# A hand-written VectorE and ScalarE order in the memory block's output projection, and another order of the FFN's PSUM banks

## The chip, the cores and the metric

The kernel runs on one core of one Trainium2 chip. The metric is the device time of one execution in microseconds (us). Before the change it was measured in three runs: 1961.02, 1964.95 and 1965.83 us, median 1964.95 us. Inside a core TensorE (PE) multiplies matrices into PSUM, VectorE (DVE), ScalarE (ACT) and GpSimd (POOL) work element by element, and SyncE (SP) issues the DMAs. Each engine executes its own instructions in a fixed order and waits on semaphores for the others.

## The reference

The reference is one decoder layer over 1024 prompt tokens and 32 sample tokens (1056 columns): a mixer, a cross-attention into 256 memory tokens, and a gated FFN with a short convolution, each added to the residual. What matters here is the end of the second and the start of the third:

```python
def mem_attend(h, mk, mv, w_mq, g_mq, w_mo):
    ...
    o = jnp.einsum('nhtm,nmhd->nthd', p, mv.astype(q.dtype)).reshape(n, t, MEM_WIDTH)
    return o @ w_mo                                   # 512 -> 1024

xp = xp + mem_attend(rms_norm(xp, g_mem_x[l]), mk, mv, w_mq[l], g_mq[l], w_mo[l])
y, buf = conv_ffn(rms_norm(xp, g_ffn[l]), ..., w_up[l], w_conv[l], b_conv[l], w_down[l])

def conv_ffn(h, buf, w_up, w_conv, b_conv, w_down):
    gate, val = jnp.split(h @ w_up, 2, axis=-1)       # 1024 -> 2 x 2816
    ...
```

All of it is float32. A float32 product is made of three products of rounded operands: each operand is split into a high part (a rounding cast) and a low part (what the cast dropped).

## The kernel before, in words

**The output projection (`out`, L1709 to L1725).** The 1056 columns are taken in two halves of 528 (`h` = 0, 1), the 1024 output rows in eight blocks of 128, `m = 4 * e + j`. One call `out(h, j, w, y)` makes two blocks (`e` = 0, 1), so the stage has 16 products; this text numbers them 0 to 15 in the order of the program: half 0 with j = 0, 1, 2, 3 (products 0 to 7), half 1 with j = 1, 2, 3, 0 (products 8 to 15). Product k is 24 matmuls of 264 columns into one of three PSUM buffers `y` of two banks each, so product k + 3 needs the buffer of product k. Then follow, on other engines:

- sum k: VectorE adds the PSUM result to the old residual, `res`, L1721 (three buffers, loaded by SP at L1715);
- SP stores the new residual to DRAM, `yd`, L1722;
- ScalarE scales it by the FFN's norm gain into `y` (L1723), and squares it (L1517 or L1520, in `square`); GpSimd adds the square to the sum of squares `ya` (L1521). The sum of squares starts anew at products 0 and 8.

The weights of one `j` (`weight(j)`, L1598) are loaded and split by `stream`: one cast on ScalarE (L190), one subtraction on VectorE (L191), 128x1024 each. Three pairs of buffers hold them, so j = 3 comes after product 1 is done, and j = 0 of the second half after product 9.

**The operand steps (`operands`, L1789).** The FFN multiplies with a Strassen-Winograd scheme: seven products of quarter blocks in the place of eight. For each half and each pair of j (d = 0: j = 0, 1; d = 1: j = 2, 3) seven operands (`FORMS`) are made from the scaled residual, four of them differences. One operand is: a difference for t1, t3, t2, t4 (VectorE, L1797, in place in `y`), the cast to the high part (ScalarE, L190) and the subtraction that gives the low part (VectorE, L191), all 128x528. That makes four blocks of seven operands, 11 VectorE instructions and 7 casts each. In this text block a is half 0, d = 0; b is half 0, d = 1; c is half 1, d = 1; d is half 1, d = 0. Blocks b and c share the buffer `y1[1]`.

**The first FFN weights (`weights`, L1816).** From two loads of `w_up` GpSimd makes four sums `s12`, `s34` (L1836 to L1840); casts and subtractions give the high and low parts of `raw[0]`, `s12`, `s34` (the last subtraction on GpSimd, L1825) and of `a22` (L1843, L1844).

**The first FFN block (`block`, L1865).** Per half seven products of 12 matmuls: A, X (t2), X (b21), F (t1, t3), E (b22, t4). Before the second X buffer can be used again, VectorE must have made `z` from the first (L1874). The second half's first product in the program as it runs is X of `t21`, which needs the operand t2 of blocks c and d.

**What sets the order.** A planner orders the instructions when the program is built: an instruction goes to its engine when its inputs are ready in the planner's own timing, the earlier one in the program first. Inside `manual_schedule(engines=...)` the named engines keep the order of the program; instructions from behind such a block may be placed into its gaps. Before the change the whole stage was left to the planner. PSUM has eight banks; a pool gives them out by the order in which its tags are first asked for. The projection's pool has `y` in banks 0 to 5 and `st` in bank 6; product 15 lies in banks 0 and 1. The FFN's pool had A in banks 0 and 1, X in 2 and 3, F in 4 and 5, E in 6 and 7.

Of the kernel before, what the change touches and what calls it, by code (L numbers as in the profile page):

```python
# [5 lines left out]
F32 = mybir.dt.float32  # L6
# [3 lines left out]
ALU = mybir.AluOpType  # L10
# [3 lines left out]
P = 128  # L14
# [10 lines left out]
HT, QT = 528, 264  # L25
# [128 lines left out]
class Net:  # L154
# [1358 lines left out]
    def square(self, p, acc, x, m):  # L1513
        nc = self.nc
        n = x.shape[1]
        if m == 0:
            nc.scalar.activation(acc, x, AF.Square)  # L1517
        else:
            sq = self.t(p, [P, max(n, 384)], F32, "sqx", 3 if n <= 384 else 2)[:, :n]
            nc.scalar.activation(sq, x, AF.Square)  # L1520
            nc.gpsimd.tensor_tensor(acc, acc, sq, ALU.add)  # L1521


    def mem_attention(self, xh, xl, r3):
        nc, tc, I, O = self.nc, self.tc, self.I, self.O
        pq = self.open("pq")
        pp = self.open("psa", space=PSUM)
# [20 lines left out]
        w, st = {}, {}  # L1548
# [149 lines left out]
        px = self.open("xo0", side="right")  # L1698
# [3 lines left out]
        y1 = [self.t(pc, [P, 2, 2, HT], F32, f"y{d}") for d in range(2)]  # L1702
        acc = self.t(self.pw, [P, 640], F32, "ya")
        pc0 = self.open("pc0", side="right")
        nc.gpsimd.memset(acc[:, HT:], 0.0)
        self.close("psa")
        pp = self.open("psm", space=PSUM)

        def out(h, j, w, y):  # L1709

            o = h * HT
            for e in range(2):
                m = 4 * e + j
# [7 lines left out]
                nc.vector.tensor_tensor(r, ps, r, ALU.add)  # L1721
                nc.sync.dma_start(self.y_dram[:, m, o : o + HT], res)  # L1722
                nc.scalar.activation(y[:, e, j % 2], res, AF.Copy, scale=self.col("g_ffn", m))  # L1723
                self.square(pc0, acc[:, :HT], res, count[0] % 8)
                count[0] += 1  # L1725

        count = [0]
        ys = self.t(pc0, [P, 2, 2, HT], F32, "y"), y1[1]
        for j in range(4):
            if j == 3:  # L1730
                w[j] = weight(j)
            out(0, j, w[j], ys[j // 2])
            if j % 2:
                self.operands(ys[j // 2], j // 2, ops[0], self.FORMS)
        r = self.t(self.pw, [P, 10], F32, "hr")

        def sums(h, st):
            for i in range(5):
                nc.tensor.matmul(st[:, i : i + 1], acc[:, i * P : i * P + P], self.ones[:, :1], start=True, stop=True)
            nc.scalar.copy(r[:, 5 * h : 5 * h + 5], st[:, :5])  # L1740

        sums(0, self.t(pp, [P, 512], F32, "st", 1))
        w[0] = weight(0)
        for j in (1, 2, 3, 0):
            out(1, j, w[j], y1[j // 2])
            if j in (3, 0):
                self.operands(y1[j // 2], j // 2, ops[1], self.FORMS[:3])
            if j == 2:
                first = self.weights(0, 1)
        self.close("pq")  # L1750
        self.close("pc0")
        px = self.open("xo2")
        rows = [self.t(px, [P, HT], F32, f"row{h}") for h in range(2)]
        for n in self.FORMS[3:]:
            form(px, 1, n)
        for d in (1, 0):
            self.operands(y1[d], d, ops[1], self.FORMS[3:])
        self.close("psm")
        self.close("pc")

        def norm(h, new):

            if h == 0:
                sums(1, new())
# [24 lines left out]
    def operands(self, y, d, ops, forms):  # L1789

        nc = self.nc
        b11, b12, b21, b22 = self.quarters(y)
        src = {"b11": b11, "b21": b21, "b22": b22, "t1": b11, "t3": b12, "t2": b22, "t4": b21}
        sums = {"t1": (b12, b11), "t3": (b22, b12), "t2": (b22, b11), "t4": (b21, b22)}
        for n in forms:
            if n in sums:
                nc.vector.tensor_tensor(src[n], *sums[n], ALU.subtract)  # L1797
# [16 lines left out]


    def weights(self, fa, fb, more=None):  # L1816

        nc, I, p = self.nc, self.I, self.pw

        def halves(src, eng=nc.vector):  # L1820
            self.nw += 1
            q = None if self.nw % 4 else more
            hi, lo = (self.t(q or self.wp, [P, 8, P], FR, x, 1 if q else None) for x in ("hi", "lo"))
            nc.scalar.copy(hi, src)  # L1824
            eng.tensor_tensor(lo, src, hi, ALU.subtract)  # L1825
# [10 lines left out]
        add(s12[:, :4], a21, a22, ALU.add)  # L1836
        add(s12[:, 4:], s12[:, :4], a11, ALU.subtract)
        w.update(zip(("s1", "s2"), halves(s12)))
        add(s34[:, :4], a11, a21, ALU.subtract)
        add(s34[:, 4:], a12, s12[:, 4:], ALU.subtract)  # L1840
        w.update(zip(("s3", "s4"), halves(s34, nc.gpsimd)))
# [4 lines left out]
        return w  # L1846

    def ffn(self, *a):
        self.ffn_up(*a)
# [2 lines left out]
    def ffn_up(self, ops, rows, norm, first):  # L1852

        nc, I, O = self.nc, self.I, self.O
        p = self.open("pf")
        pp = self.open("psf", space=PSUM)
        state = self.t(p, [P, NF, 16], F32, "state")
        nc.sync.dma_start(state, I["state"])
        conv = self.t(p, [P, NF, 18], F32, "conv")
        ocol, wcol = COL["b_conv"][0], COL["w_conv"][0]  # L1860
        def product(ps, a, b):
            pairs = lambda x: [(x[0][:, k], x[1][:, k]) for k in range(4)]
            self.mm3(ps, pairs(a), pairs(b))
# [87 lines left out]
        for q in range(NF // 2):  # L1951
            fs = 2 * q, 2 * q + 1
            w = self.weights(*fs, p) if q else first
# [4 lines left out]
            w = self.weights(NF + fs[0], NF + fs[1], p)  # L1958
# [128 lines left out]
```

## Time and profile before

| | |
|---|---|
| median of 3 runs | 1964.95 us |
| the profiled execution | 1963.94 us, span 1961.9 us from its first to its last instruction |
| TensorE busy | 1882.0 us, 96% of the span |
| VectorE busy | 1372.2 us, 70% |
| ScalarE, GpSimd busy | 902.1 us, 705.0 us |
| the output projection's first matmul | at 1167.87 us |
| the FFN's first matmul, `A` | at 1225.26 us |
| the first matmul of the FFN's second half, `X<-t21h` | at 1242.67 us |

A row of the timeline gives the start in us, the duration in us, the engine, the line, the operation, output and inputs, and in brackets how long the engine sat idle before it and which instruction released it. SPq is SyncE's queue of DMA issues. Each matmul row counts from its own start to the modelled end, so rows overlap; the distance of two starts is what one matmul takes of the engine. A row of windows gives the busy time of each engine in a stretch, and PEclk, the granted TensorE clock as a share of full speed.

### The profile page before, as it was taken

How to read it: one execution, taken by the hardware profiler on the slowest of the kernel's cores; microseconds unless marked ns; L12 is line 12 of the kernel's file. 1: busy time of each engine (PE TensorE's matmuls, PEld its weight loads, DVE VectorE, ACT ScalarE, POOL GpSimd, SP SyncE). 2: the span in 40 equal slices, each digit the busy share in tenths (PEclk: the TensorE clock that was granted, in tenths of full speed). 3: DMA queues.
4: the chain of work that ended last, by engine and by line, in shares of the span. 5: the costliest groups of instructions: out<-in, count | busy, mean ns of one | idle time of the engine just before them, and what ended most of it. 6: DMA issues, size and time to landing. Idle time of an engine off the chain costs nothing.

```text
span 1961.9 us, 40154 instructions
## 1 busy us (share of the span) xinstructions
PE 1882.0 (96%) x14556; PEld 1770.0 (90%) x14556; DVE 1372.2 (70%) x2949; ACT 902.1 (46%) x1880; POOL 705.0 (36%) x811
## 2 busy tenths in 40 slices
PE   5999899999999999999999998899999999999999
PEld 5999778768888989888899978899999999899999
DVE  8774867766777767777655668888888988832521
ACT  6334667666555555555533556433333333521311
POOL 5230401003544444444133015467677676100000
PEclk9999899999999999999999999899999999999999
DMA  5101100106865665654565145122222222754642
GB/s 202 50 5 49 57 1 2 61 14 184 223 181 162 176 176 170 173 166 136 172 186 180 37 152 184 40 78 79 86 66 77 88 75 90 213 171 128 200 124 66
DMA packets 130312, 229.42 MB, mean 117 GB/s; under 512 B 20449, under 2 KB 86850, under 8 KB 130114
## 3 DMA queue, kind: packets, MB, share of 16 engines
q1 hardware_dynamic: 129250, 225.81, 37.9%
q8 instruction: 115, 1.88, 0.4%
q10 hardware_dynamic: 864, 1.05, 0.2%
q14 instruction: 83, 0.68, 0.1%
HBM read 195.13 MB, written 31.66 MB: 116 GB/s over the span
## 4 chain that ended last, share of the span: by engine, by line
PE 67%; DVE 8%; issue 5%; DMA 4%; POOL 2%; ACT 1%; SPq 1%; POOLq 0%; DVEq 0%; ACTq 0%
PE s L184 14%; PE d L184 13%; PE b L184 7%; PE X L184 6%; PE F L184 6%; PE E L184 6%; PE A L184 3%; PE o L847 2%; PE tp L834 2%; PE tp L184 1%; DMA araw<-actd 1%; PE o L1277 1%; DMA cT<-cT 1%; DVE mx L1228 1%; PE tp L789 1%
## 5 line engine op out<-in xcount | busy, mean ns | idle before, releaser
L184 PE MATMUL s<-w2h,ch 128*128 128x288 f32 (+1 forms) x1024 | 305.9, 299 | 0.0
L184 PE MATMUL s<-w2h,cl 128*128 128x288 f32 (+1 forms) x1024 | 295.0, 288 | 2.8 <-POOL cl L1164 2.0
L184 PE MATMUL s<-w2l,ch 128*128 128x288 f32 (+1 forms) x1024 | 294.7, 288 | 0.0
L184 PE MATMUL d<-a,hi 128*128 128x264 f32 x1408 | 260.5, 286 | 3.4 <-DVE a L191 1.7
L184 PEld LDWEIGHTS d<-a,hi 128*128 128x128 f32 x1408 | 219.6, 189 | 5.2 <-DVE a L191 3.2
L184 PEld LDWEIGHTS s<-w2h,ch 128*128 128x128 f32 x1024 | 192.6, 188 | 19.1 <-issue 13.6
L184 PE MATMUL d<-a,lo 128*128 128x264 f32 x704 | 200.3, 285 | 0.0
L184 PEld LDWEIGHTS s<-w2h,cl 128*128 128x128 f32 x1024 | 192.4, 188 | 3.5 <-POOL cl L1164 2.3
L184 PEld LDWEIGHTS s<-w2l,ch 128*128 128x128 f32 x1024 | 192.8, 188 | 0.0
L1207 DVE TENSOR_REDUCE ss<-sq 128x16 f32<-128x1024 f32 x128 | 155.4, 1214 | 48.4 <-ACT sq L1204 48.2
L191 DVE TENSOR_TENSOR lo<-raw,hi 128x1024 fp32r<-128x1024 f32 (+1 forms) x71 | 83.3, 1174 | 131.3 <-ACT hi L190 131.2
L190 ACT CAST hi<-raw 128x1024 fp32r<-128x1024 f32 (+1 forms) x71 | 71.0, 1000 | 180.8 <-PE d L184 157.3
L1164 POOL TENSOR_TENSOR cl<-cT,ch 128x512 fp32r<-128x512 f32 x64 | 83.6, 1306 | 167.1 <-ACT ch L1160 148.5
L184 PEld LDWEIGHTS d<-a,lo 128*128 128x128 f32 x704 | 133.0, 189 | 0.0
L1204 ACT ACTIVATE sq<-s 128x512 f32<-128x512 f32 x128 | 76.6, 598 | 90.9 <-PE s L184 90.9
L1201 ACT ACTIVATE sq<-s 128x512 f32<-128x512 f32 x128 | 76.7, 599 | 82.9 <-PE s L184 82.6
L184 PE MATMUL mm<-whi,xh 128*128 128x256 f32 (+3 forms) x288 | 85.1, 297 | 11.0 <-ACT xh L194 11.0
L184 PE MATMUL mm<-whi,xl 128*128 128x256 f32 (+3 forms) x288 | 83.0, 299 | 7.1 <-DVE xl L197 7.1
L1521 POOL TENSOR_TENSOR acc<-acc,sqx 128x384 f32<-128x384 f32 (+1 forms) x42 | 45.9, 1093 | 110.8 <-ACT sqx L1520 109.8
L1825 POOL TENSOR_TENSOR lo<-s,hi 128x1024 fp32r<-128x1024 f32 x22 | 68.9, 3131 | 45.9 <-ACT hi L1824 45.9
L184 PE MATMUL mm<-wlo,xh 128*128 128x256 f32 (+3 forms) x288 | 84.9, 296 | 0.0
L1160 ACT CAST ch<-cT 128x512 fp32r<-128x512 f32 x128 | 73.5, 628 | 4.1 <-DMA cT<-cT 4.1
(656 smaller groups left out, 6194.4 us busy)
## 6 DMA issues: line engine op xcount, KB each, us to landing
cT<-cT SPq DMA_DIRECT2D x256, 160.0 KB, 2.5
ck<-ck SPq DMA_DIRECT2D x256, 144.0 KB, 3.2
raw<-w_up SPq DMA_DIRECT2D x44, 512.0 KB, 3.6
raw<-w_down SPq DMA_DIRECT2D x32, 512.0 KB, 3.8
actd<-cv SPq DMA_DIRECT2D x44, 264.0 KB, 2.2
araw<-actd SPq DMA_DIRECT2D x44, 264.0 KB, 4.0
raw<-w_down SPq DMA_DIRECT2D x16, 384.0 KB, 3.3
res<-res SPq DMA_DIRECT2D x16, 264.0 KB, 3.2
```

Source lines behind the costliest of these rows:

```text
L184: self.nc.tensor.matmul(out, l, r, start=first and i == 0, stop=last and i == len(seq) - 1)
L190: {"act": nc.scalar.copy, "pool": nc.gpsimd.tensor_copy, "dve": nc.vector.tensor_copy}[eng](hi, src)
L191: low = lambda: nc.vector.tensor_tensor(lo, src, hi, ALU.subtract)
L834: nc.tensor.transpose(tp[:, z * P : z * P + P], u[e][:, jj * P : jj * P + P], self.ident)
L847: nc.tensor.matmul(u["o"][jj * 64 : jj * 64 + 64, c], s["v"][:, j + jj, h % 4], th[:, jj * 256 : jj * 256 + c.stop - c.start], start=j == ...
L1160: nc.scalar.copy(d["h"][:, k], src[k])
L1164: (nc.vector if k else nc.gpsimd).tensor_tensor(d["l"][:, k], src[k], d["h"][:, k], ALU.subtract)
L1201: nc.scalar.activation(sq[:, 0], ps[:, :, n0 : n0 + 256], AF.Square)
L1204: nc.scalar.activation(sq[:, 1], pt.rearrange("p (e d) -> p e d", e=2), AF.Square)
L1207: yield lambda: nc.vector.tensor_reduce(s["ss"][:, g0 : g0 + 2].rearrange("p e (z h) -> p z e h", z=2), sq.rearrange("p z e (h d) -> p z e ...
L1521: nc.gpsimd.tensor_tensor(acc, acc, sq, ALU.add)
L1825: eng.tensor_tensor(lo, src, hi, ALU.subtract)
```

## The change

VectorE and ScalarE get the order of the program from product 0 to the last operand step. To give them a good text to follow, the operand steps become a generator (`operands` yields after each operand, and its low part is issued one operand late), and `steps(n)` issues n of them. Each `out` call now issues, for each of its two products, the sum, the store, the scaling, the square of the product before (no longer its own), and then two operand steps if any block is waiting (four during j = 1 of the second half). Blocks a and b are so spread over products 4 to 7 and 8 to 9; three operands of block c follow products 14 and 15; the last four of c and all of d come at the end. The split of j = 3's weights moves from in front of product 6 to in front of product 4, that of the second half's j = 0 from in front of product 8 to in front of product 10. The first FFN weights are taken in three parts: loads, `raw[0]` and `s12`'s sums in front of product 12; the split of `s12` and `s34`'s sums behind product 13; the rest behind product 15. In `ffn_up` six tiles are asked for in the order E, X, X, F, A, A before they are used, so E gets banks 0 and 1, X 2 and 3, F 4 and 5, A 6 and 7. No computation is added or left out.

```diff
@@ out @@
-                self.square(pc0, acc[:, :HT], res, count[0] % 8)
+                square()
+                old.append(res)
+                steps(4 if (h, j) == (1, 1) else 2)
+
+        count, work, old = [0], [], []
+
+        def square():
+            if old:
+                self.square(pc0, acc[:, :HT], old.pop(), count[0] % 8)
                 count[0] += 1
+        def steps(n):
+            while n and work:
+                if next(work[0], self) is self:
+                    work.pop(0)
+                else:
+                    n -= 1
@@ the loops @@
-        for j in range(4):
-            if j == 3:
-                w[j] = weight(j)
-            out(0, j, w[j], ys[j // 2])
-            if j % 2:
-                self.operands(ys[j // 2], j // 2, ops[0], self.FORMS)
...
-            nc.scalar.copy(r[:, 5 * h : 5 * h + 5], st[:, :5])
-        sums(0, self.t(pp, [P, 512], F32, "st", 1))
-        w[0] = weight(0)
-        for j in (1, 2, 3, 0):
-            out(1, j, w[j], y1[j // 2])
-            if j in (3, 0):
-                self.operands(y1[j // 2], j // 2, ops[1], self.FORMS[:3])
-            if j == 2:
-                first = self.weights(0, 1)
...
+            return lambda: nc.scalar.copy(r[:, 5 * h : 5 * h + 5], st[:, :5])
+        with self.tc.manual_schedule(engines={mybir.EngineType.DVE, mybir.EngineType.Activation}):
+            for j in range(4):
+                if j == 2:
+                    w[3] = weight(3)
+                out(0, j, w[j], ys[j // 2])
+                if j % 2:
+                    work.append(self.operands(ys[j // 2], j // 2, ops[0], self.FORMS))
+            square()
+            copy = sums(0, self.t(pp, [P, 512], F32, "st", 1))
+            for j in (1, 2, 3, 0):
+                if j == 2:
+                    steps(99)
+                    copy()
+                    w[0] = weight(0)
+                if j == 3:
+                    it = self.weights_steps(0, 1)
+                    next(it)
+                out(1, j, w[j], y1[j // 2])
+                if j == 3:
+                    next(it)
+                    work.append(self.operands(y1[1], 1, ops[1], self.FORMS[:3]))
+            square()
+            steps(99)
+            first = [x for x in it][-1]
...
+            work.append(self.operands(y1[1], 1, ops[1], self.FORMS[3:]))
+            work.append(self.operands(y1[0], 0, ops[1], self.FORMS))
+            steps(99)
@@ operands @@
-            self.split(*(x[:, 2 * d : 2 * d + 2] for x in ops[n]), src[n])
+            hi, lo = (x[:, 2 * d : 2 * d + 2] for x in ops[n])
+            nc.scalar.copy(hi, src[n])
+            if old:
+                nc.vector.tensor_tensor(*old, ALU.subtract)
+            old = lo, src[n], hi
+            yield
+        nc.vector.tensor_tensor(*old, ALU.subtract)
@@ weights becomes weights_steps, with a yield behind s12's and behind s34's sums @@
@@ ffn_up @@
+        for tag, n, k in (("E", 2, 1), ("X", 1, 2), ("X", 1, 2), ("F", 2, 1), ("A", 1, 2), ("A", 1, 2)):
+            self.t(pp, [P, n, 512] if n > 1 else [P, 512], F32, tag, k)
```

More of the change, by code (lines that the diff above doesn't have):

```diff
@@ L1723, in out @@
                 nc.scalar.activation(y[:, e, j % 2], res, AF.Copy, scale=self.col("g_ffn", m))
-                self.square(pc0, acc[:, :HT], res, count[0] % 8)
-                count[0] += 1
-        count = [0]
-        ys = self.t(pc0, [P, 2, 2, HT], F32, "y"), y1[1]
-        for j in range(4):
-            if j == 3:
-                w[j] = weight(j)
-            out(0, j, w[j], ys[j // 2])
-            if j % 2:
-                self.operands(ys[j // 2], j // 2, ops[0], self.FORMS)
+                square()
[5 more added lines that the diff above has]
+                self.square(pc0, acc[:, :HT], old.pop(), count[0] % 8)
+                count[0] += 1
+        def steps(n):
[4 more added lines that the diff above has]
+                    n -= 1
+        ys = self.t(pc0, [P, 2, 2, HT], F32, "y"), y1[1]
         r = self.t(self.pw, [P, 10], F32, "hr")
@@ L1739, in sums @@
                 nc.tensor.matmul(st[:, i : i + 1], acc[:, i * P : i * P + P], self.ones[:, :1], start=True, stop=True)
-            nc.scalar.copy(r[:, 5 * h : 5 * h + 5], st[:, :5])
-        sums(0, self.t(pp, [P, 512], F32, "st", 1))
-        w[0] = weight(0)
-        for j in (1, 2, 3, 0):
-            out(1, j, w[j], y1[j // 2])
-            if j in (3, 0):
-                self.operands(y1[j // 2], j // 2, ops[1], self.FORMS[:3])
-            if j == 2:
-                first = self.weights(0, 1)
[L1750 to L1757, printed above, removed]
+            return lambda: nc.scalar.copy(r[:, 5 * h : 5 * h + 5], st[:, :5])
[23 more added lines that the diff above has]
+            first = [x for x in it][-1]
+            self.close("pq")
+            self.close("pc0")
+            px = self.open("xo2")
+            rows = [self.t(px, [P, HT], F32, f"row{h}") for h in range(2)]
+            for n in self.FORMS[3:]:
+                form(px, 1, n)
+            work.append(self.operands(y1[1], 1, ops[1], self.FORMS[3:]))
+            work.append(self.operands(y1[0], 0, ops[1], self.FORMS))
+            steps(99)
         self.close("psm")
@@ L1763, in norm @@
             if h == 0:
-                sums(1, new())
+                sums(1, new())()
                 self.rsqrt(self.pw, r, r, 1.0 / 1024)
@@ L1794, in operands @@
         sums = {"t1": (b12, b11), "t3": (b22, b12), "t2": (b22, b11), "t4": (b21, b22)}
+        old = None
         for n in forms:
@@ L1816, in weights, with weights_steps @@
     def weights(self, fa, fb, more=None):
+        return [w for w in self.weights_steps(fa, fb, more)][-1]
+    def weights_steps(self, fa, fb, more=None):
         nc, I, p = self.nc, self.I, self.pw
@@ L1837, in weights @@
         add(s12[:, 4:], s12[:, :4], a11, ALU.subtract)
+        yield
         w.update(zip(("s1", "s2"), halves(s12)))
@@ L1840, in weights @@
         add(s34[:, 4:], a12, s12[:, 4:], ALU.subtract)
+        yield
         w.update(zip(("s3", "s4"), halves(s34, nc.gpsimd)))
@@ L1845, in weights @@
         w["a22"] = hi, lo
-        return w
+        yield w
     def ffn(self, *a):
```

## The prediction

> **What bounds the kernel now.** I read the page first, then the windows around the stage that the diff touches, then each engine's timeline there.
>
> ```profile
> span 1961.9 us, 40154 instructions
> PE 1882.0 (96%) x14556; PEld 1770.0 (90%) x14556; DVE 1372.2 (70%) x2949; ACT 902.1 (46%) x1880; POOL 705.0 (36%) x811
> ```
>
> ```profile
> 1185.00:1210.00 25.00, 22.54 (x184) 22.12 (x183) 24.68 (x29) 16.04 (x27) 12.11 (x9) 1.00 0.59 187
> 1210.00:1226.00 16.00, 9.56 (x76) 9.38 (x76) 12.76 (x12) 10.28 (x17) 10.63 (x8) 0.93 0.57 180
> 1226.00:1242.00 16.00, 13.18 (x93) 13.09 (x91) 15.80 (x18) 6.85 (x14) 7.74 (x6) 0.82 0.09 28
> 1265.00:1330.00 65.00, 65.00 (x521) 65.00 (x522) 55.15 (x74) 21.48 (x28) 41.63 (x37) 0.97 0.20 67
> ```
>
> Overall TensorE is the bound, and from 1265 us on it is full, so a shift of the FFN's start goes to the end undiminished. In the stage itself it is VectorE: busy 24.68 of 25 us and 15.80 of 16 us in two of the first three stretches, while TensorE has holes. Where they are, the timeline of TensorE says:
>
> ```profile
> 1167.87 0.29 PE L184 MATMUL y<-qh,hi 128*128 128x264 f32 x1
> ...
> 1170.79 0.28 PE L184 MATMUL y<-qh,hi 128*128 128x264 f32 x1
> ...
> 1225.26 0.56 PE L184 MATMUL A<-b110h,hi 128*128 128x264 f32 x1 [6.44 <-DVE res L1721]
> ...
> 1242.67 0.59 PE L184 MATMUL X<-t21h,hi 128*128 128x264 f32 x1 [3.49 <-DVE z L1874]
> ```
>
> Product 15 ends at 1225.26 - 6.44 = 1218.82 us. A then waits 6.44 us for sum 15, whose PSUM banks it takes over, and the second half's first product waits 3.49 us more for VectorE. The first two rows are 24 matmuls apart: a product takes 2.92 us.
>
> ```profile
> 1174.86 1.23 DVE L191 TENSOR_TENSOR lo<-raw,hi 128x1024 fp32r<-128x1024 f32 x1 [0.25 <-ACT hi L190]
> ...
> 1187.71 1.79 DVE L191 TENSOR_TENSOR b220l<-y,b220h 128x528 fp32r<-128x528 f32 x1
> ...
> 1207.46 0.69 DVE L1721 TENSOR_TENSOR res<-y,res 128x528 f32<-128x528 f32 x1
> ...
> 1224.42 0.69 DVE L1721 TENSOR_TENSOR res<-y,res 128x528 f32<-128x528 f32 x1
> ...
> 1226.15 2.89 DVE L191 TENSOR_TENSOR b111l<-y,b111h 128x528 fp32r<-128x528 f32 x1
> ...
> 1237.48 0.70 DVE L191 TENSOR_TENSOR t31l<-y,t31h 128x528 fp32r<-128x528 f32 x1
> 1238.10 0.70 DVE L191 TENSOR_TENSOR t21l<-y,t21h 128x528 fp32r<-128x528 f32 x1
> ...
> 1241.19 0.70 DVE L191 TENSOR_TENSOR t41l<-y,t41h 128x528 fp32r<-128x528 f32 x1
> ...
> 1242.18 0.43 DVE L1874 TENSOR_TENSOR z<-X,a 128x264 f32<-128x264 f32 x1
> ```
>
> ```profile
> 1180.26 1.77 POOL L1836 TENSOR_TENSOR s<-raw 128x512 f32<-128x512 f32 x1
> ...
> 1187.18 1.76 POOL L1840 TENSOR_TENSOR s<-raw,s 128x512 f32<-128x512 f32 x1
> ...
> 1209.65 1.33 POOL L1521 TENSOR_TENSOR ya<-ya,sqx 128x528 f32<-128x528 f32 x1 [0.93 <-ACT sqx L1520]
> ...
> 1225.62 2.85 POOL L1825 TENSOR_TENSOR lo<-s,hi 128x1024 fp32r<-128x1024 f32 x1
> ```
>
> These are VectorE's and GpSimd's timelines. Two low parts in a row are 0.62 us apart (1237.48, 1238.10). Beside GpSimd the same instruction takes 1.79: it ends at 1189.50, 0.56 after GpSimd's instruction of 1187.18 ended. The one at 1226.15 ends 0.57 us after GpSimd's of 1225.62. So a 128x528 instruction on two SBUF tensors doesn't run beside GpSimd's; the two take turns, and each turn of GpSimd costs VectorE about 1.1 us (1.72 against 0.62), its 128x1024 subtraction 2.2. The residual sums, which read PSUM, are spared:
>
> ```profile
> L1797 DVE TENSOR_TENSOR y<-y 128x528 f32<-128x528 f32 x16 | 18.8, 1179 | 0.5
> L1721 DVE TENSOR_TENSOR res<-y,res 128x528 f32<-128x528 f32 x16 | 11.2, 698 | 5.9 <-PE y L184 5.9
> ...
> L1521 POOL TENSOR_TENSOR ya<-ya,sqx 128x528 f32<-128x528 f32 x14 | 21.5, 1535 | 34.0 <-ACT sqx L1520 34.0
> ```
>
> ScalarE's spacings, from its timeline: scaling 0.64 us, square 0.54, 528-column cast 0.52, 1024-column cast 0.94.
>
> ```profile
> 1209.41 1.03 ACT L1824 CAST hi<-raw 128x1024 fp32r<-128x1024 f32 x1
> 1210.35 0.73 ACT L1723 ACTIVATE y<-res,cols 128x528 f32<-128x528 f32 x1
> 1210.99 0.63 ACT L1520 ACTIVATE sqx<-res 128x528 f32<-128x528 f32 x1
> ...
> 1218.32 0.63 ACT L1520 ACTIVATE sqx<-res 128x528 f32<-128x528 f32 x1
> 1218.86 0.62 ACT L190 CAST b211h<-y 128x528 fp32r<-128x528 f32 x1
> 1219.38 0.63 ACT L190 CAST b221h<-y 128x528 fp32r<-128x528 f32 x1
> ```
>
> **The change part by part.** No instruction is added or dropped on any engine, so the sum is one of order. I walk the new program order with these durations up to the point that decides, the start of X<-t21h (1242.67 now).
>
> *Weights of j = 3.* Now split at 1174.86, while VectorE had nothing else. In the new text the split stands behind sum 3. Product 3 ends at 1167.87 + 4 x 2.92 = 1179.6; sum 3 ends near 1180.5; scaling 3, square 2 and the cast take until 1182.7; the subtraction waits out GpSimd's addition of square 2 and ends at 1184.1; sum 4, ready since 1182.7, ends at 1184.8. TensorE needs these weights at product 6 (1185.4), so this costs it nothing yet. The next weight load, which takes over the raw buffer, is issued on SP after 1184, not 1176, and GpSimd's four weight additions (first one 1180.26 now) move to about 1188 to 1196, into the operand steps.
>
> *Blocks a and b.* From 1184.8 VectorE has in a row: 22 operand instructions at 0.62 = 13.6; sums 5 to 9, 3.1; nine turns of GpSimd (squares 3 to 7, four weight additions) at 1.1 = 9.9; and waits for ScalarE, which in the program's order has scaling and square ahead of each block's first cast: 0.64 + 0.54 + 0.62 = 1.8 for block a, 1.3 for b (no square is due there), 0.7 at a's last low part. That is 30.4. Two or three of GpSimd's turns fall into those waits or beside a sum (-2.8). Block b ends near 1212.4. The four-step rule puts all of it ahead of sum 10, and so does the split of j = 0's weights (cast to 1212.6, subtraction to 1213.8). Sum 10 ends at 1214.5; now it ends at 1207.46 + 0.69 = 1208.15. Product 13 needs its PSUM buffer: it starts at 1214.5 where it now starts at 1218.82 - 3 x 2.92 = 1210.1. Product 15 ends 4.4 us later, at 1223.3.
>
> *The last sums.* The split of `raw[0]` stands ahead of sum 12 and waits for scaling, square, scaling, square (2.4) and its own cast after sum 10; that of `s12` stands ahead of sum 14 in the same way. Sums 12 and 13 end at 1220.1 and 1220.7; 2.4 of ScalarE, the cast 1.03 and the subtraction 1.4 put the end of sum 14 at 1225.7, though product 14 is done at 1220.6. Ahead of sum 15 stands block c's first low part: 1.8 of ScalarE and a turn of GpSimd's; sum 15 ends at 1229.85. Now it ends at 1225.11: +4.7.
>
> *The tail.* Behind sum 15 ScalarE has scaling, square, cast, square, the `s34` cast and the `a22` cast, 0.64 + 2 x 0.54 + 2 x 0.52 + 0.94 = 3.7; VectorE reaches the `a22` subtraction (1181 before, hidden) near 1234.3. Then 8 differences and 11 low parts, 19 x 0.62 = 11.8, and GpSimd's subtraction (2.2 to 2.9) and two weight additions (1.1 each): 1251.5. Now the last low part ends at 1241.89: 16.8 us behind sum 15 against 21.6, or +4.8. Last comes z, 0.4: X<-t21h near 1251.9, 9.3 us later than 1242.67 (4.7 + 4.8, less 0.2 since z now waits 0.3 behind the last low part).
>
> *The bank order.* A no longer waits for sum 15, and 6.44 us of hole vanish there. But A, the rest of the half (7 products of 12 matmuls, 10.2 us) and the ten small matmuls are done by about 1243 even where F waits for GpSimd's `s34` low part until 1237.5; after them X<-t21h waits for the operands anyway. The hole moves behind the first half and grows from 3.49 to about 9 us. Worth of this part: 0, and up to 1.5 if the planner pulls the 12 matmuls of the second half's A into the hole.
>
> *SP.* The square of product k now follows scaling k + 1, so each residual load is released a product later. In the walk the loads for sums 12 and 13 land 0.2 to 0.7 us ahead of use: cover, but thin.
>
> Behind X<-t21h the same work follows in the same order, with two smaller holes that wait for VectorE as before:
>
> ```profile
> 1258.63 0.39 PE L1778 MATMUL A<-ident,hr 16*128 16x16 f32 x2 [0.91 <-ACT a L1870]
> ...
> 1264.85 0.59 PE L184 MATMUL X<-t20h,hi 128*128 128x264 f32 x1 [2.56 <-DVE z L1874]
> ```
>
> The sum: 1963.94 + 9.3 = 1973.2 for the profiled execution, whose time is 1.0 below the median; between the two I take 1973.5. Unknown are GpSimd's and SP's orders, which the planner sets anew; moving GpSimd's weight additions and subtraction about in the walk changes it by 0 to +4, the pulled-in A by -1.5, an early z by -1: own range 1968.5 to 1979.
>
> **The rivals.** *Faster: VectorE is not held by GpSimd.* If GpSimd's turns fall into VectorE's waits, each operand instruction costs 0.62. Then blocks a and b end near 1204, sum 10 is on time, product 15 ends near 1216, sum 15 near 1220, and the tail of 3.7 + 11.8 gives X<-t21h near 1235: -7.8, or 1956. For it: low parts that find GpSimd idle run at 0.70, as those of 1237.48 and 1238.10. Against it: the 16 differences average 1.18 us, and GpSimd's additions of squares come at every product. Between the two lie 17.1 us, so it decides from where fewer than about 45% (7.8 of 17.1) of GpSimd's turns cost VectorE their 1.1 us.
>
> [...]
>
> *No change.* The paired work of VectorE and GpSimd is the same, and an order alone may leave its end where it is: VectorE's idle time before 1218 in the trace would be used instead of lost, and only the tail's 4.8 us of waits and leftover instructions stay, less the 1 to 1.5 us of A and z: 1964 to 1969. Against it stand the waits for scaling and square, 1.8 us at each block's start.
>
> *Still slower: the residual's round trip.* The chain of waits already runs through it:
>
> ```profile
> 1208.18 5.40 DMA yd<-res
> ...
> 1213.64 2.77 DMA res<-res
> ```
>
> If store and load take these times behind the later square, sums 12 to 15 slip by 2 to 6 us more: 1977 to 1982.
>
> **How the numbers follow.** The walk 0.62, faster 0.16, no change 0.14, still slower 0.08. A measurement of this kernel tells about 0.3% (5.9 us) from no change. The walk's lower end lies inside that bound, so a part of its chance goes there: faster 0.17, same 0.15, slower 0.68. The range from 1959 to 1980 leaves out most of the faster case and a part of the slowest.
>
> **What would show it.** Sum 10 near 1214 and product 15 ending near 1223; a run of VectorE from 1185 to 1212 with about 1.7 us per operand instruction beside GpSimd; A starting at once behind product 15; sums 14 and 15 about 5 us behind their products; a hole of some 9 us ahead of X<-t21h, which starts near 1252; no new hole behind 1270. The prediction is wrong if sum 10 comes before 1210 or X<-t21h before 1247.

## The result and the profile after

The changed kernel takes 1969.47 us (median of 12 runs, 1963.89 to 1970.65), the kernel before 1962.78 us beside it on the same chip (12 runs). The ratio, which goes by the means of the runs, is 1.0024, 95% interval [1.0014, 1.0033]; the medians lie 0.34% apart. So the change made the kernel a little slower, by less than the forecast. The profiled execution took 1970.65 us. From the page of the changed kernel, the span and the engines' busy time:

```profile
span 1968.6 us, 40153 instructions
...
PE 1882.4 (96%) x14556; PEld 1771.6 (90%) x14556; DVE 1369.0 (70%) x2949; ACT 900.6 (46%) x1880; POOL 703.8 (36%) x811
```

The work is the same to a few instructions. TensorE's timeline in the stage has other holes (start, duration, engine, line, operation, and in brackets the idle time and what ended it):

```profile
1217.04 0.39 PE L184 MATMUL y<-qh,hi 128*128 128x264 f32 x1 [3.54 <-DVE res L1721]
...
1225.29 0.39 PE L184 MATMUL y<-qh,hi 128*128 128x264 f32 x1 [0.61 <-DVE res L1721]
...
1228.33 0.28 PE L184 MATMUL A<-b110h,hi 128*128 128x264 f32 x1
...
1231.38 0.36 PE L184 MATMUL X<-t20h,hi 128*128 128x264 f32 x1 [1.43 <-DVE res L1721]
...
1257.06 2.58 PE L1804 MATMUL A<-ident,hr 128*128 128x128 f32 x10 [9.34 <-DVE hr L230]
1259.57 0.59 PE L184 MATMUL X<-t21h,hi 128*128 128x264 f32 x1
...
1293.24 0.28 PE L184 MATMUL A<-b110h,hi 128*128 128x264 f32 x1
```

Product 13 waits 3.54 us for sum 10, product 15 waits 0.61 us for sum 12 (it needs its PSUM buffer), A follows product 15 at once, and the long hole of 9.34 us now lies ahead of the ten matmuls of the half-row (`half_row`, L1804 here), which run directly ahead of X<-t21h. The last row is A of the second step of the FFN's loop, called A of q = 1 below. VectorE's timeline of the same kernel:

```profile
1172.68 0.71 DVE L1721 TENSOR_TENSOR res<-y,res 128x528 f32<-128x528 f32 x1 [2.10 <-PE y L184]
...
1216.29 1.31 DVE L1721 TENSOR_TENSOR res<-y,res 128x528 f32<-128x528 f32 x2
1220.48 1.74 DVE L1862 TENSOR_TENSOR lo<-raw,hi 128x1024 fp32r<-128x1024 f32 x1 [2.87 <-ACT hi L1861]
1224.53 0.71 DVE L1721 TENSOR_TENSOR res<-y,res 128x528 f32<-128x528 f32 x1 [2.32 <-DMA res<-res]
1226.05 0.71 DVE L1721 TENSOR_TENSOR res<-y,res 128x528 f32<-128x528 f32 x1 [0.81 <-DMA res<-res]
1229.11 1.51 DVE L1862 TENSOR_TENSOR lo<-s,hi 128x1024 fp32r<-128x1024 f32 x1 [2.35 <-ACT hi L1861]
1230.54 0.69 DVE L1721 TENSOR_TENSOR res<-y,res 128x528 f32<-128x528 f32 x1
1233.83 0.70 DVE L1721 TENSOR_TENSOR res<-y,res 128x528 f32<-128x528 f32 x1
...
1255.72 0.70 DVE L1832 TENSOR_TENSOR t41l<-y,t41h 128x528 fp32r<-128x528 f32 x1
1256.74 0.17 DVE L230 SCALAR_TENSOR_TENSOR hr<-rqa,rqy 128x10 f32<-128x10 f32 x1
1256.92 0.43 DVE L1916 TENSOR_TENSOR z<-X,a 128x264 f32<-128x264 f32 x1
```

These are sums 0, 10 and 11, the split of `raw[0]`, sums 12 and 13 (each waiting for its residual load), the split of `s12`, sums 14 and 15, the last low part, the last instruction of the norm's rsqrt (`hr`) and `z`. Of the kernel before, sum 0 on VectorE and A of q = 1 on TensorE are still missing above:

```profile
1170.99 0.71 DVE L1721 TENSOR_TENSOR res<-y,res 128x528 f32<-128x528 f32 x1 [2.09 <-PE y L184]
```

```profile
1284.03 0.28 PE L184 MATMUL A<-b110h,hi 128*128 128x264 f32 x1
```

Sum 0 itself starts 1.7 us later after the change, where nothing was changed yet; over all kernels below it starts between 1169.7 and 1174.2. So every time from here on counts from the start of sum 0. The columns are the starts of sums 10 and 15, the end of the last low part, the starts of X<-t21h and of A of q = 1, and the time between these two; the last column is the ratio to the kernel before, with its interval.

| kernel | sum 10 | sum 15 | last low ends | X<-t21h | A, q = 1 | between | ratio |
|---|---|---|---|---|---|---|---|
| before | 36.5 | 53.4 | 70.9 | 71.7 | 113.0 | 41.4 | 1 |
| after | 43.6 | 61.2 | 83.7 | 86.9 | 120.6 | 33.7 | 1.0024 [1.0014, 1.0033] |
| e1 banks only | 36.5 | 52.5 | 70.0 | 70.8 | 112.4 | 41.6 | 0.9994 [0.9985, 1.0003] |
| e2 order only | 43.6 | 61.0 | 83.7 | 86.8 | 120.4 | 33.6 | 1.0030 [1.0020, 1.0040] |
| e3 own square | 45.4 | 62.8 | 84.0 | 84.9 | 127.9 | 43.0 | 1.0079 [1.0066, 1.0092] |
| e4 planner free | 36.5 | 52.5 | 70.0 | 70.8 | 112.4 | 41.6 | 1.0007 [0.9999, 1.0016] |
| e5 row early, before | 36.5 | 52.5 | 69.9 | 74.8 | 107.0 | 32.2 | 0.9960 [0.9946, 0.9973] |
| e6 z first | 43.6 | 60.3 | 82.4 | 82.8 | 124.4 | 41.6 | 1.0054 [1.0040, 1.0068] |
| e7 four residuals | 43.9 | 59.9 | 82.5 | 85.7 | 118.5 | 32.9 | 1.0009 [0.9999, 1.0019] |
| e8 no square sums | 40.1 | 56.3 | 78.0 | 81.2 | 114.1 | 33.0 | 0.9999 [0.9989, 1.0010] |
| e9 own square, four | 45.3 | 61.0 | 82.8 | 83.8 | 126.2 | 42.4 | 1.0059 [1.0044, 1.0074] |
| e10 splits behind | 43.8 | 60.5 | 87.8 | 89.8 | 125.0 | 35.2 | 1.0064 [1.0048, 1.0080] |
| e11 block b later | 42.0 | 60.6 | 82.8 | 83.8 | 125.2 | 41.5 | 1.0068 [1.0053, 1.0083] |
| e12 banks and row | 36.5 | 52.5 | 70.0 | 76.1 | 109.9 | 33.8 | 0.9975 [0.9965, 0.9985] |
| e13 loads and splits | 45.3 | 59.0 | 85.2 | 87.2 | 120.8 | 33.6 | 1.0036 [1.0024, 1.0048] |
| e14 row early, banks | 36.5 | 52.7 | 70.1 | 79.1 | 111.3 | 32.2 | 0.9999 [0.9989, 1.0008] |

In e6 the record of A's first matmul is missing; its time is that of the X twelve matmuls later, less the 1.46 us that these take after the change.

The first two rows say where the time went: X<-t21h is 15.2 us later, of which 7.7 come back before A of q = 1. From there to the last product of the FFN both kernels take the same (409.8 us). The down projection is 2.5 us shorter after the change. 1.7 (ahead of sum 0) + 15.2 - 7.7 - 2.5 = 6.7 us, the difference of the spans.

### The profile page after: what moved, and what is told of

It reads as the page before. It is cut to its first block, busy times and chain, and to the rows that moved or that the text cites. A ratio compares the mean times of both kernels' runs of the same rounds, so it can differ in the third digit from the quotient of the medians.

```text
span 1968.6 us, 40153 instructions
## 1 busy us (share of the span) xinstructions
PE 1882.4 (96%) x14556; PEld 1771.6 (90%) x14556; DVE 1369.0 (70%) x2949; ACT 900.6 (46%) x1880; POOL 703.8 (36%) x811
```

## The experiments

**Which part carries the loss.** The change has two parts that can be made alone, the banks (e1) and the hand-written order (e2); e4 keeps the new text but leaves the order to the planner.

```diff
e1, on the kernel before (ffn_up):
+        for tag, n, k in (("E", 2, 1), ("X", 1, 2), ("X", 1, 2), ("F", 2, 1), ("A", 1, 2), ("A", 1, 2)):
+            self.t(pp, [P, n, 512] if n > 1 else [P, 512], F32, tag, k)
e2, on the changed kernel: these two lines taken out
e4, on the changed kernel:
-        with self.tc.manual_schedule(engines={mybir.EngineType.DVE, mybir.EngineType.Activation}):
+        if True:
```

> The kernel before with the FFN's bank order alone; the planner still orders VectorE and ScalarE. Theory 1, that VectorE's operand steps decide the start of the second half's first product: A starts at once behind product 15 (the 6.4 us hole goes), X of t21 still starts within 1 us of 74.8 us behind the projection's first matmul, and the time is that of before within 2 us. Theory 2, that the bank order has worth of its own, because the norm's small matmuls move into the hole and the down projection's first banks come free differently: 3 to 8 us faster than before.

> The changed kernel with the FFN's banks in the old order. If the hand-written order makes all of the loss and the banks are worth nothing: the time of the changed kernel within 2 us. If the banks give back a part (2.5 us in the down projection, and more by letting the norm come early): 3 to 8 us slower than the changed kernel, 1972 to 1977.

> The changed kernel's text with VectorE and ScalarE left to the planner. If the fixed order on the two engines makes the loss (each waits for the other in turn): sum 10 back near 40 us behind the first matmul, and the time that of before or faster, 1957 to 1963. If the new text itself is to blame (later splits, later squares): slower than before by 3 us or more.

Measured: 1963.85, 1969.53 and 1965.55 us beside 1964.73 of the kernel before. TensorE's timeline of e1, at the first half's A, at X<-t21h and at the first matmul of the down projection:

```profile
1219.23 0.28 PE L184 MATMUL A<-b110h,hi 128*128 128x264 f32 x1
...
1242.34 0.59 PE L184 MATMUL X<-t21h,hi 128*128 128x264 f32 x1 [8.93 <-DVE z L1877]
...
1698.06 0.48 PE L184 MATMUL d<-a,hi 128*128 128x264 f32 x2 [4.00 <-DVE G L1947]
```

The bank order does what it says, A no longer waits 6.44 us, and most of the hole goes to X<-t21h, where VectorE decides (8.93 against 3.49). At the other end it puts a wait ahead of the down projection, whose first bank is now E's; even so the time from the last E to the end is 267.7 us in e1 and 268.1 in the kernel before. So the banks are worth nothing in the kernel before (e1) and in the changed one (e2); e14 below has a kernel in which they cost time. The text without the order is worth nothing either (e4 has e1's times to 0.1 us up to A of q = 1); its 1965.55 us lie above the range expected of it, but are not clear of the kernel before. The whole loss is the hand-written order's.

**What comes back behind X<-t21h.** e3 was made for another question: it gives each product its own square again, which should release the residual buffers earlier.

```diff
-                square()
                 old.append(res)
+                square()
                 steps(4 if (h, j) == (1, 1) else 2)
```

> The changed kernel with each product's square right behind its own scaling, as before the change. If the late release of the residual buffers makes sums 12 and 13 late (both waited for their load in the changed kernel): the load of residual 12 is issued some 6 us earlier, sum 12 no longer waits for it, product 15 ends about 3 us earlier, and the time falls by 2 to 3 us. If the order of sums, splits and steps alone sets product 15's end: no change within 1 us.

Measured: 1979.48 us, ten more than the changed kernel, though X<-t21h comes 2 us earlier; neither of the two forecasts came true. TensorE's timeline of e3:

```profile
1256.63 0.59 PE L184 MATMUL X<-t21h,hi 128*128 128x264 f32 x1 [8.94 <-DVE z L1916]
...
1263.60 1.37 PE L1804 MATMUL A<-ident,hr 128*128 128x128 f32 x10
...
1276.52 0.59 PE L184 MATMUL X<-t20h,hi 128*128 128x264 f32 x1 [4.55 <-DVE z L1916]
```

The half-row stands behind X<-t21h again, as in the kernel before, and with it a hole comes back. In the column "between" of the table the kernels fall into two groups, 32 to 35 us and 41 to 43 us. In all kernels of the first group the half-row's ten matmuls run ahead of X<-t21h, in all of the second behind it. The reason can be read on VectorE. In the kernel before:

```profile
1254.38 1.37 DVE L1910 TENSOR_TENSOR G<-G,row 128x1056 f32<-128x1056 f32 x1 [2.51 <-ACT row L1781]
...
1264.38 0.42 DVE L1874 TENSOR_TENSOR z<-X,a 128x264 f32<-128x264 f32 x1
```

and in the changed kernel:

```profile
1260.50 1.26 DVE L1952 TENSOR_TENSOR G<-G,row 128x1056 f32<-128x1056 f32 x1
...
1265.66 0.43 DVE L1916 TENSOR_TENSOR z<-X,a 128x264 f32<-128x264 f32 x1
```

The gate is multiplied by the row, then convolved on VectorE, and the next `z`, which frees the X bank, stands behind that. Before, the row is multiplied 11.7 us behind the start of X<-t21h, and `z` comes 10 us later, too late for TensorE (the 2.56 us wait that the prediction shows, and the slow matmuls behind it). After, the row is there 0.9 us behind X<-t21h and `z` 5.2 us later, in time. Not all of the 7.7 us is a gain: the ten matmuls, 1.3 us in the kernel before, and a part of the slow matmuls behind a long hole (granted clock 0.50 from 1257.06 to 1262.60 after the change) have only moved ahead of X<-t21h. The two holes (0.91 and 2.56 us) and the slow matmuls behind the second (1.4 us) are gone, 4.9 us together. Three experiments move the row, and e5 with it the sums of squares behind it (the code of all three is shortened):

```diff
e5, on the kernel before (behind the allocation of the rows, ahead of the last operand steps):
+        st = lambda: self.t(pp, [P, 512], F32, "st", 1)
+        sums(1, st())
+        self.rsqrt(self.pw, r, r, 1.0 / 1024)
         for d in (1, 0):
             self.operands(y1[d], d, ops[1], self.FORMS[3:])
...
-            if h == 0:
-                sums(1, new())
-                self.rsqrt(self.pw, r, r, 1.0 / 1024)
e6, on the changed kernel (gate), the rsqrt behind z:
+            if (fs[0], h) == (0, 0):
+                with self.tc.manual_schedule(engines={mybir.EngineType.DVE}):
+                    block(w, ops[h], place)
+                    norm(h, lambda: self.t(pp, [P, 512], F32, "A", 2))
...
e12, on e1 (block, gate), the rsqrt ahead of z:
+            if (fs[0], h) == (0, 0):
+                with self.tc.manual_schedule(engines={mybir.EngineType.DVE}):
+                    block(w, ops[h], place, row1)
...
```

In e12 `row1` is the call of `norm`, which `block` now makes behind the copy of A.

> The kernel before, with its own stage; only the second half's sums of squares, their five matmuls and the rsqrt are issued ahead of the last operand steps instead of inside the first FFN block. In the program the half-row's matmuls then stand ahead of X<-t21 on TensorE, as in the changed kernel, and not behind 50 matmuls of the second half. Theory place (the 7.7 us that the changed kernel regains behind X<-t21 come from where the row is made): X<-t21 starts 0 to 3 us later than in the kernel before, no hole behind it, from X<-t21 to the next A<-b110 of q=1 34 to 36 us instead of 41.4, time 1957 to 1961. Rival slack (they come from VectorE having caught up during the 9 us hole): the holes of 0.91 and 2.56 us stay in some form, 1964 to 1968.

> The changed kernel with VectorE's order written out for the first FFN block too: z, G and zz of the first half first, then the rsqrt. The operand stage is unchanged. Theory place: X<-t21 starts 2 to 4 us earlier than in the changed kernel (about 88 us, not 90, behind the first product), but the half-row falls behind it, holes come back behind X<-t21 and 41 to 43 us pass from there to the A<-b110 of q=1, so that the time is 1972 to 1977. Rival slack: the 33.7 us stay, and the time falls by the 2 to 4 us, to 1965 to 1968.

> The kernel before with the changed kernel's bank order, and with VectorE's order in the first FFN block written out so that the rsqrt stands ahead of z; the half-row then stands ahead of X<-t21 on TensorE. Unlike e5_row_early_before, the first half's products do not stand behind the sums of squares. Theory place: X<-t21 2 to 4 us later than in e1_banks_only, 32 to 35 us from there to q=1, time 1955 to 1959. Rival (the gain of e5_row_early_before came from something else, the moved sums): 1962 to 1965.

Measured: 1956.31, 1974.33 and 1959.71 us. TensorE's timeline of e5, the fastest of all:

```profile
1228.02 2.29 PE L1739 MATMUL st<-ones,ya 128*128 128x1 f32 x10 [10.46 <-POOL ya L1521]
...
1243.10 1.48 PE L1778 MATMUL A<-ident,hr 128*128 128x128 f32 x10
1244.51 0.40 PE L184 MATMUL X<-t21h,hi 128*128 128x264 f32 x1
...
1276.75 0.28 PE L184 MATMUL A<-b110h,hi 128*128 128x264 f32 x1
```

and of e6:

```profile
1253.26 0.59 PE L184 MATMUL X<-t21h,hi 128*128 128x264 f32 x1 [8.55 <-DVE z L1916]
...
1260.78 1.37 PE L1804 MATMUL A<-ident,hr 128*128 128x128 f32 x10
...
1274.55 0.59 PE L184 MATMUL X<-t20h,hi 128*128 128x264 f32 x1 [2.93 <-DVE z L1916]
```

e5 leaves the stage of the kernel before as it is (sums 10 and 15 as in e1) and loses 3.1 us at X<-t21h, but saves 9.1 behind it: 6.0 us earlier at A of q = 1, and no hole on TensorE from A on. e6 wins 4.1 us at X<-t21h and loses 7.9 behind it: 3.8 us later at A of q = 1. Both came out as theory place had it, e5 even 0.7 us below its range; the rival, that VectorE had merely caught up during the long hole, falls, since e6 and e3 have a hole of 8.5 us and more ahead of X<-t21h and still wait behind it. e12 lies just outside (X<-t21h 5.3 us later than in e1, not 2 to 4). Its row of the half-row's matmuls shows where it loses 1.1 us to e5:

```profile
1245.00 2.58 PE L1778 MATMUL A<-ident,hr 128*128 128x128 f32 x10 [8.59 <-DVE hr L230]
```

TensorE stands idle for 8.59 us ahead of them and runs them in 2.58 us; in e5, where the first half's products are late and fill that time, they take 1.48. Counted at A of q = 1, the row's place was worth 6.0 us in e5, 3.8 in e6 and, in e12 against e1, 2.5.

e14 puts the new banks under e5.

> The kernel of e5_row_early_before with the changed kernel's bank order. Theory (the bank order is worth nothing, the row's place is worth 6 to 8 us): 1955 to 1959, within 2 us of e5_row_early_before. Rival (with the other bank order the gain of the row's place shrinks, as e12_banks_and_row with 1959.7 may mean): 1959 to 1961.

Measured: 1962.49 us, beyond the rival's range, with the same 32.2 us between but X<-t21h 4.3 us later than in e5. TensorE's timeline of e14 names the cause:

```profile
1238.55 0.59 PE L184 MATMUL A<-b110h,hi 128*128 128x264 f32 x1 [5.11 <-ACT hr L1740]
```

With E in banks 0 and 1, A lies in the banks 6 and 7, bank 6 being that of `st`, and waits until ScalarE has copied the sums from there. The bank order took one wait for a bank away and made another.

**Why X<-t21h is late.** Sum 10 is 7.1 us later after the change, sum 15 7.7, the last low part 12.8. e8 takes out GpSimd's additions of squares, e11 moves the split for products 14 and 15 from ahead of sum 10 to ahead of sum 12. It was meant to move the rest of block b as well, but nothing is left of it there: at four operands for each of products 8 and 9 all seven of block b are issued ahead of sum 10 in both kernels, and `steps(99)` finds no work.

```diff
e8 (square):
-                self.square(pc0, acc[:, :HT], old.pop(), count[0] % 8)
+                x = old.pop()
+                d = acc[:, :HT] if count[0] % 8 == 0 else self.t(pc0, [P, HT], F32, "sqx", 2)
+                nc.scalar.activation(d, x, AF.Square)
e11:
-                if j == 2:
+                if j == 3:
                     steps(99)
                     copy()
                     w[0] = weight(0)
-                if j == 3:
                     it = self.weights_steps(0, 1)
```

> The changed kernel without GpSimd's 14 additions of squares in the projection's stage; the squares are still computed on ScalarE, but not summed, so the norm's row holds other numbers. Theory turns (each turn of GpSimd costs VectorE 1.1 us of an operand step): five of them fall away ahead of sum 10, which comes 4 to 5.5 us earlier than 46.7 us behind the first product, X<-t21 5 to 8 us earlier, time 1961 to 1965. Rival casts (VectorE waits for ScalarE's casts and for its place behind the products): sum 10 moves by less than 2 us, time 1967 to 1969.

> The changed kernel with the rest of block b and the split of the weights of products 14 and 15 ahead of sum 12 instead of sum 10. Theory (the products are late, but do not decide): sum 10 comes 3 to 5 us earlier than 46.7 us behind the first product and product 13 with it, sum 15 and X<-t21 stay within 1.5 us of 64.3 and 90.0. Rival (the late sum 10 is passed on to the end): sum 15 and X<-t21 come 3 to 5 us earlier. The half-row's matmuls fall behind X<-t21 here, as in e3_own_square, so by theory place 41 to 43 us pass from X<-t21 to q=1 and the time is 1973 to 1980, or 1969 to 1974 by the rival of the sums.

Measured: 1963.9 and 1977.32 us. In e8 sum 10 comes 3.6 us earlier, a little less than expected (0.7 us for each of the five additions that the forecast counts ahead of it, not 1.1), sum 15 4.9 and X<-t21h 5.7. The turns of GpSimd are the largest single price that was found in the stage. Taking away 14 GpSimd instructions made VectorE's stage 5.7 us shorter, so they cost VectorE time, 0.4 us each on the mean. In e11 sum 10 gains only 1.6 us, not 3 to 5: that is the split and the wait for its cast, since block b has stayed where it was. Sum 15 gains 0.6. X<-t21h gains 3.1, of which 2.2 are the half-row that is no longer ahead of it (3.2 us from the last low part to X<-t21h after the change, 1.0 in e11). With so small a move of sum 10, and 1.0 us of it left at the last low part, this run does not tell its two theories apart.

The last sums: e7 and e9 give the residual a fourth buffer, e10 puts the splits of `raw[0]` and `s12` behind sum 15 (in the program's text also their loads and GpSimd's sums), e13 does both.

```diff
e7, on the changed kernel; e9, on e3 (out):
-                res = self.t(pc0, [P, HT], F32, "res", 3)
+                res = self.t(pc0, [P, HT], F32, "res", 4)
e10, on the changed kernel; e13, on e9:
                     it = self.weights_steps(0, 1)
-                    next(it)
                 out(1, j, w[j], y1[j // 2])
                 if j == 3:
-                    next(it)
```

> The changed kernel with four residual buffers instead of three: TensorE, VectorE, ScalarE and GpSimd keep their order, SP issues each residual load one store earlier. Theory round trip (sums 12 and 13 wait for loads that are issued only when a store beside the 512 KB weight load has landed): no wait for a residual load, sum 12 ends near 1223 and sum 13 near 1224, sums 14 and 15 and X<-t21 2 to 3 us earlier, time 1966 to 1968. Rival split order (the casts and subtractions of the weights ahead of sums 12 and 14 set the pace anyway): sum 15 and X<-t21 move by less than 1 us, 1969 to 1970.

> The kernel of e3_own_square with four residual buffers instead of three: TensorE, VectorE, ScalarE and GpSimd keep that kernel's order, and SP issues the loads for sums 12 and 13 ahead of the 512 KB weight load instead of behind it. Theory round trip: no wait for a residual load; sum 13 follows sum 12 within a microsecond (near 55 us behind the first product instead of 58.05), sum 15 near 63.5 instead of 65.9, X<-t21 near 86 instead of 88.1, time 2 to 3 us below that of e3_own_square, 1976 to 1978. Rival split order: sum 15 and X<-t21 move by less than 1 us, time 1978.5 to 1980.

> The changed kernel with the splits of raw[0] and s12 behind sum 15 instead of ahead of sums 12 and 14. Theory one (the splits hold the last sums, but VectorE has the same work ahead of it in any order): sum 15 comes 3 to 5 us earlier than 64.3 us behind the first product, the last low part and X<-t21 move by less than 1.5 us, time 1967 to 1971. Rival (the late last sums are what makes the tail late): the last low part and X<-t21 come 3 to 5 us earlier, time 1964 to 1966.

> The kernel of e9_own_square_four (own square, four residual buffers) with, in addition, the splits of raw[0] and s12 behind sum 15 as in e10_splits_behind: both things that hold the last sums are taken away at once. Counted from the start of sum 0, sum 15 stands at 61.15 us in the changed kernel, 61.02 in e9_own_square_four, 60.48 in e10_splits_behind. Theory two limits side by side (loads and splits each hold the last sums to about the same time, so that taking away one alone shows little): sum 15 comes at 53 to 57. Rival (VectorE and ScalarE are simply full there): sum 15 stays at 59 or later. Both: the time is not better than that of the changed kernel by more than 2 us, since the splits then lengthen the tail as in e10_splits_behind.

Measured: 1966.65, 1976.86, 1976.92 and 1970.44 us. VectorE's rows of sums 12 and 13 in e7,

```profile
1223.94 0.69 DVE L1721 TENSOR_TENSOR res<-y,res 128x528 f32<-128x528 f32 x1
1226.39 0.71 DVE L1721 TENSOR_TENSOR res<-y,res 128x528 f32<-128x528 f32 x1 [1.76 <-issue]
```

in e9,

```profile
1225.33 1.31 DVE L1721 TENSOR_TENSOR res<-y,res 128x528 f32<-128x528 f32 x2
```

of sums 12, 13 and 14 in e10,

```profile
1225.33 1.39 DVE L1721 TENSOR_TENSOR res<-y,res 128x528 f32<-128x528 f32 x2 [6.31 <-DMA res<-res]
1230.43 0.71 DVE L1721 TENSOR_TENSOR res<-y,res 128x528 f32<-128x528 f32 x1 [3.71 <-DMA res<-res]
```

and of sum 14 in e13:

```profile
1226.78 0.71 DVE L1721 TENSOR_TENSOR res<-y,res 128x528 f32<-128x528 f32 x1 [3.60 <-DMA res<-res]
```

In e7 only the load for sum 12 is early; the one for sum 13 still stands behind a weight load on SP. Sum 15 comes 1.2 us earlier, X<-t21h 1.2. In e9 both loads are early, sum 13 follows sum 12 at once and 3.1 us earlier than in e3, as expected; but of these 3.1 only 1.8 reach sum 15 and 1.2 X<-t21h. So the loads, whose waits the changed kernel shows as 2.32 and 0.81 us, were worth 1.2 to 1.8 us, between the two theories. e10 shows what stands beside them: without the splits the sums wait 6.31 and 3.71 us for loads instead, sum 15 gains 0.7 us (not the 3 to 5 expected), and the tail behind it grows from 22.6 to 27.3 us; its time is above the ranges of both its theories. In e13 sum 12 follows sum 11 at once, but then product 13 and the load for sum 14 decide; sum 15 comes at 59.0, the rival's bound, 2.2 us before the changed kernel's. The last sums have three limits within some 2 us of each other, and what is taken from in front of sum 15 is paid behind it.

## Why the prediction was right or wrong

The direction was right and the size too large: 1973.5 us were forecast against 1969.47, +0.4% against +0.24%. X<-t21h came 5.9 us later than forecast, and what followed was 7.7 and 2.5 us quicker. These errors cancel in good part, so that the time lies as near the forecast as it does is luck.

- *Weights of j=3*: right. Sum 4 ended at 1186.7, less 1.7 for the later sum 0, or 1185.0; forecast 1184.8.
- *Blocks a and b*: right. Sum 10 is 7.1 us later, forecast 6.3. The GpSimd turns in it are real, if cheaper than charged (e8: 0.7 us each, not 1.1), and the rival *Faster*, which needed most of them to cost nothing, falls.
- *The last sums*: the term was +4.7 and measured +7.7. 0.8 of the 3.0 is sum 10's, if that is passed on whole (e11 leaves it open). 1.2 to 1.8 are the residual loads (e7, e9). *SP* had called their cover thin, 0.2 to 0.7 us, and charged nothing; it was missing, by 2.3 and 0.8 us. The rival *Still slower* named this mechanism, at 2 to 6 us. The remaining 0.4 to 1.0 us weren't found.
- *The tail*: right. The last low part ends 22.6 us behind the start of sum 15 against 17.5, +5.1; forecast +4.8.
- From the last low part to X<-t21h 0.2 us less were forecast, and it took 2.4 more (3.2 against 0.8): the half-row, at half the clock after the hole (0.50 from 1257.06 to 1259.57), stands there now. With the two above, 3.0 + 0.3 + 2.6 = 5.9, X<-t21h is 15.2 us late and not 9.3.
- *The bank order*: right, worth nothing (e1, e2), and the planner pulled no A into the hole.
- "Behind X<-t21h the same work follows in the same order, with two smaller holes": this is the step that failed. The order was not the same, and the holes went: the same move of the half-row that costs 2.6 us ahead of X<-t21h saves 7.7 behind it (e3, e5, e6: 8 to 9 us behind X<-t21h between one place and the other). It was nowhere in the diff: the planner placed the row anew behind the hand-written part. Why it put it ahead in e2 and e7 and behind in e3, the runs don't show. "No new hole behind 1270" was right, but for the wrong reason: the old holes had gone too.
- That a shift "goes to the end undiminished" held from A of q = 1 to the last product of the FFN (409.8 us in both kernels), not behind it: the down projection's 2.5 us were not forecast. Over all kernels the time from the last E to the end lies between 265.1 and 268.8 us, with either bank order at both ends (265.6 in e2, 268.8 in e4). What decides it stays open.

The measured time lies 0.5 us above the range of the rival *No change*, but not by its mechanism: the order alone did cost 15 us in the stage.

## What to carry to other kernels

An order written by hand for two engines also changes what a planner does with the instructions behind it; compare the whole program order of both versions, and look for short dependent chains that feed a later stage. Here a chain of thirteen tiny instructions and ten small matmuls (the norm's row) was worth 2.5 to 6 us by its place (e12, e6, e5), and moving it ahead in the old kernel (e5, 0.9960 [0.9946, 0.9973]) beats both versions. The length of a wait in the profile is not its price: of 3.1 us waited for loads 1.2 to 1.8 were to be had, since the next limit stood close behind.

## What the runs showed of the hardware

In the kernel before TensorE's granted clock was 0.50 right behind the hole of 2.56 us. Windows there and then further on (busy times of the engines, then the granted clock, the DMA share and GB/s):

```profile
1264.85:1267.60 2.75, 2.75 (x12) 2.75 (x13) 2.61 (x5) 0.38 (x1) 2.11 (x1) 0.50 0.51 191
1267.60:1270.00 2.40, 2.40 (x19) 2.40 (x18) 1.34 (x4) 1.50 (x2) 0.87 (x6) 0.86 0.00 0
```

For about 3 us a matmul of 264 columns takes 0.22 us instead of 0.12 (the distances of the starts from 1265.24 to 1268.10, and from 1268.30 on). In e5, behind a hole of 1.74 us ahead of product 8, the granted clock was 1.00:

```profile
1191.90:1194.90 3.00, 3.00 (x24) 3.00 (x25) 2.99 (x4) 2.95 (x5) 1.33 (x1) 1.00 0.39 146
```

But the length of the hole alone doesn't decide what follows right behind it. After the change and in e2 a hole of 2.63 us stands ahead of product 10. After the change the granted clock behind it was 0.50 from 1201.86 to 1204.66 and 1.00 from 1204.81 to 1207.50, and the first two matmuls last 0.59 and 0.42 us; in e2 they last 0.39 and 0.29, as the first two behind e5's hole of 1.74 us do at a granted clock of 1.00. The rows, after the change and then in e2:

```profile
1201.86 0.59 PE L184 MATMUL y<-qh,hi 128*128 128x264 f32 x1 [2.63 <-DVE res L1721]
1202.24 0.42 PE L184 MATMUL y<-ql,hi 128*128 128x264 f32 x1
```

```profile
1200.78 0.39 PE L184 MATMUL y<-qh,hi 128*128 128x264 f32 x1 [2.63 <-DVE res L1721]
1201.01 0.29 PE L184 MATMUL y<-ql,hi 128*128 128x264 f32 x1
```

In e3, behind a hole of 2.24 us ahead of a matmul of F, the first four matmuls start 0.23, 0.12 and 0.13 us apart, and the next ones 0.22 (granted clock 0.56 from 1240.76 to 1244.50). What decides stays open. In the kernel before the hole of 2.56 us cost its length and some 1.4 us more (14 matmuls at 0.1 us).
